# A weight-load counter that starts at three, and one weight split moved ahead of small work, in a two-layer encoder trunk

## The chip, the core and the metric

The kernel runs on one core of a Trainium2 chip. The core has TensorE (PE; its weight loads are shown as PEld), VectorE (DVE), ScalarE (ACT), GpSimd (POOL) and SyncE (SP, here only an issuer of DMAs). Each engine takes its instructions in the order in which the program was written for it. The metric is the time of one execution on the device in microseconds. A change of the time is told apart from none, for this kernel, only if it is above about 0.3%.

## What is computed

The input is x of 256 positions by 2048 features, in float32. Two layers are applied, each an attention with a residual and then a squared-ReLU MLP with a residual; between them one shared key/value projection is made for the second layer.

```
u = rms_norm(h, a_norm_g);  proj = u @ a_w_in            # q, k, v and 16 forget gates
q, k = rms_norm per head;   logf = log_sigmoid(fz + b_f) # layer a: 16 heads of 128
s = q k^T * scale + c[t] - c[s]   (c = cumsum logf, causal);  o = softmax(s) v
h = h + o @ a_w_out;  h = h + relu(rms_norm(h) @ w1)^2 @ w2       # 2048 -> 8192 -> 2048
k_sh, v_sh = rms_norm(h) @ kv_w                                    # shared by layer b
q = rms_norm(rms_norm(h) @ b_w_q);  s = q k_sh^T * scale + rel_bias (own chunk + 8 before)
h = h + softmax(s) v_sh @ b_w_out;  h = h + relu(rms_norm(h) @ w1')^2 @ w2'
```

About 0.5 GB of float32 weights are read once, and every weight has to be multiplied at float32 accuracy.

## The kernel before, in words

**Stages.** The program is one straight stream. In the profiled execution the q/k/v projection of layer a with its attention lies at about 0 to 290 us, the projection after the attention (`w_oa`) up to about 380, the MLP of layer a and the query projection of layer b up to about 1045, the shared key/value projection with the attention of layer b and its output projection up to about 1405, and the MLP of layer b to the end.

**Units and splits.** Weights are worked through in units of 128x1024 float32 elements. A unit is split by ACT into a rounded part `hi` (L339) and by DVE into the rest `lo` (L340); PE then makes three passes with it, `hi` by the high part of the activations (L608), `hi` by their low part (L610) and `lo` by the high part (L612), four matmuls of 512 columns in each pass. `hi` and `lo` have three buffers each. So the split of a unit can start only when PE has done with the unit three before it: `hi` is free after the L610 pass and `lo` after the L612 pass.

**Pairs and forms.** Two panels of 512 output columns make a pair. Part of the products of a pair is saved by a seven-product scheme for 2x2 blocks: instead of eight block products there are seven, on sums of the weight blocks. These sums are called forms (names "11", "T3", "T2", "T1", "21", "T4", "22" of L157). Some sums are made by DVE (L990, L992), others by a DMA from POOL's queue that adds a second weight block into the tile where the first lies (L1005, L1007). In layer a the q/k/v projection after the first few panels goes in four pairs of the kind "three": their forms are 1536 columns wide, that is three couples of 256-row blocks. Such a form is worked in two items, first its 1024 columns (6 matmuls) and at once after that the other 512 (3 matmuls, tiles `half`); only the first is a full unit with buffers of `hi` and `lo`. Between the forms stand narrow units, of 12 matmuls each.

**Order of the work.** `plan_heads` and `plan_mlp` write down a list of items (pair, kind, number): kind 0 or 1 is a narrow unit of one of the two panels, kind 2 the first part of a form, kind 3 the second. `run` (L1025) goes through that list. At each narrow unit `fetch` calls `top_up` (L356), which splits ahead until three full units are split and not yet given to PE, and loads ahead until three raw units (four within the MLPs) wait in SBUF. Then come the unit's 12 matmuls, and after them `run_fill` (L1061) takes the next entry of a queue of small work, as often as the table `HM` says for that item. The small work is softmax, head norms, transposes through DRAM (`carry`: rows to DRAM from SP at L466, columns back at L472), the second layer's sums and so on. At a form of a "three" pair nothing is split ahead first: the form's own unit is popped, and one unit more is split only after the form's second part (`top_up(AHEAD - 1)`). All of this gives the order in which the instructions stand on PE, DVE, ACT and SP, and that order is kept.

**Where a loaded unit lies.** `load` (L300) issues the DMA of the next narrow unit on SP (L310). It counts its calls in `extra[1]`. Within the MLPs (`extra[0]` is true) each load whose count is divisible by five does not go into one of the four buffers `raw` but into one of the two buffers of the tag `z`, as `zraw`. The same two buffers take in turn the transposed tiles `z` of the hidden panels and of h; these leave by 16 small DMAs from SP and POOL (`hop`, L482) or through DRAM (L466, L472).

```
extra[1] += 1
raw = qkv.tile([P, UN], F32, name="zraw", tag="z", bufs=2) if extra[0] and extra[1] % 5 == 0 else wraw.tile([P, UN], F32, name="raw")
```

## Time and profile before

| | |
|---|---|
| median of 3 runs | 2062.64 us (2061.12 to 2068.23) |
| the profiled execution, its own time | 2057.46 us |
| its span from first to last instruction | 2055.7 us |
| PE busy | 2044.0 us, 99% of the span, 9048 matmuls |
| DVE busy | 1786.3 us, 87% |
| ACT busy | 1410.1 us, 69% |
| DMA | 560.92 MB, mean 273 GB/s |
| granted TensorE clock | 1.00 |

The profiled execution is shorter than the median by 5.2 us. A busy share is an average over the whole span. A row of the profile names the line of the kernel, the engine, the operation and "output<-input" tiles; brackets and arrows give the idle time of that engine before it and what ended that idle time. Matmuls are pipelined: one of 512 columns is shown as about 390 ns long, but in an undisturbed stream four follow each other in some 0.91 us. So a wait of PE that is short against the modelled length of a matmul can be hidden in its row.

### The profile page before, as it was taken

What the parts mean: (1) busy time and instruction counts of PE and PEld (TensorE: products, weight loads), DVE (VectorE), ACT (ScalarE), POOL (GpSimd) and SP (SyncE); (2) the same over time, 40 slices, a digit from 0 to 9 for tenths busy, and PEclk for the clock granted to TensorE, in tenths of its full rate; (3) what the DMA queues carried; (4) which work ended last, traced back from release to release, by engine and by line L of the source; (5) the groups of instructions that cost most, each with busy time, mean ns of one, the idle gap of its engine ahead of it and who ended that gap; (6) DMA issues with size and microseconds to landing.
All of it is one profiled execution on the core that took longest, in us unless ns stands there. A gap on an engine that the chain in (4) does not pass through costs nothing.

```text
span 2055.7 us, 27156 instructions
## 1 busy us (share of the span) xinstructions
PE 2044.0 (99%) x9048; PEld 1684.3 (82%) x9048; DVE 1786.3 (87%) x2099; ACT 1410.1 (69%) x1826; POOL 252.4 (12%) x359
## 2 busy tenths in 40 slices
PE   9999999999999999999999999999999999999999
PEld 8887878877888888888788888888788888888887
DVE  7888888898898899898888787888988988988996
ACT  7776666677677676667678666667766676776764
POOL 1222110011111102101012111100111111111020
PEclk9999999999999999999999999999999999999999
DMA  8899997998888898898889988878988888888985
GB/s 322 275 282 290 298 294 238 307 271 263 292 260 285 259 296 275 243 293 260 267 246 296 282 256 280 259 253 286 294 290 266 266 265 293 261 286 255 301 259 149
DMA packets 177901, 560.92 MB, mean 273 GB/s; under 512 B 40912, under 2 KB 69472, under 8 KB 155232
## 3 DMA queue, kind: packets, MB, share of 16 engines
q1 hardware_dynamic: 155552, 466.04, 63.7%
q0 software_dynamic: 21920, 92.84, 23.0%
q8 instruction: 71, 1.16, 0.2%
q14 instruction: 70, 0.57, 0.1%
q10 hardware_dynamic: 288, 0.30, 0.0%
HBM read 519.22 MB, written 27.29 MB: 266 GB/s over the span
## 4 chain that ended last, share of the span: by engine, by line
PE 89%; DMA 4%; issue 3%; DVE 2%; ACT 1%; SPq 0%; POOL 0%; DVEq 0%; ACTq 0%; POOLq 0%
PE acc L612 21%; PE acc L608 21%; PE acc L610 21%; PE s L612 8%; PE s L608 8%; PE s L610 8%; DVE lo L340 1%; DMA turn<-z 1%; PE po L745 1%; PE po L776 1%; ACT hi L339 1%; DMA wT<-in_w1fa 1%; DMA w<-in_w1fb 0%; DMA z<-turn 0%; DMA raw<-in_w1sb 0%
## 5 line engine op out<-in xcount | busy, mean ns | idle before, releaser
L339 ACT ACTIVATE hi<-raw 128x1024 fp32r<-128x1024 f32 (+1 forms) x401 | 421.5, 1054 | 197.3 <-PE acc L610 128.9
L340 DVE TENSOR_TENSOR lo<-raw,hi 128x1024 fp32r<-128x1024 f32 (+1 forms) x401 | 485.2, 1213 | 70.5 <-ACT hi L339 65.0
L608 PE MATMUL acc<-hi,act 128*128 128x512 f32 x1750 | 490.6, 393 | 2.7 <-ACT hi L339 2.6
L612 PE MATMUL acc<-lo,act 128*128 128x512 f32 x1750 | 484.8, 390 | 1.1 <-DVE lo L340 0.8
L610 PE MATMUL acc<-hi,act 128*128 128x512 f32 x1750 | 484.2, 389 | 0.0
L612 PEld LDWEIGHTS acc<-lo,act 128*128 128x128 f32 x1750 | 327.8, 188 | 72.4 <-DVE lo L340 4.5
L608 PEld LDWEIGHTS acc<-hi,act 128*128 128x128 f32 x1750 | 326.5, 188 | 71.7 <-ACT hi L339 4.8
L610 PEld LDWEIGHTS acc<-hi,act 128*128 128x128 f32 x1750 | 328.4, 188 | 69.2 <-DVE act L399 0.5
L339 ACT ACTIVATE hi<-w 128x1024 fp32r<-128x1024 f32 x254 | 266.9, 1058 | 124.6 <-PE acc L610 83.8
L340 DVE TENSOR_TENSOR lo<-wT,hi 128x1024 fp32r<-128x1024 f32 x220 | 267.1, 1221 | 63.7 <-ACT hi L339 59.8
L340 DVE TENSOR_TENSOR lo<-w,hi 128x1024 fp32r<-128x1024 f32 x254 | 305.6, 1219 | 17.4 <-ACT hi L339 15.7
L339 ACT ACTIVATE hi<-wT 128x1024 fp32r<-128x1024 f32 x220 | 232.2, 1060 | 102.5 <-PE acc L610 44.2
L608 PE MATMUL s<-hi,act 128*128 128x512 f32 x522 | 144.7, 392 | 0.5 <-ACT hi L339 0.5
L612 PE MATMUL s<-lo,act 128*128 128x512 f32 x522 | 143.3, 389 | 0.1
L610 PE MATMUL s<-hi,act 128*128 128x512 f32 x522 | 142.7, 388 | 0.0
L482 POOL DMA_DIRECT2D q<-z x192 | 95.7, 513 | 254.1 <-DVE z L456 212.5
L612 PEld LDWEIGHTS s<-lo,act 128*128 128x128 f32 x522 | 97.3, 188 | 21.8 <-DVE lo L340 2.0
L608 PEld LDWEIGHTS s<-hi,act 128*128 128x128 f32 x522 | 97.5, 188 | 21.3 <-ACT hi L339 1.4
L610 PEld LDWEIGHTS s<-hi,act 128*128 128x128 f32 x522 | 97.8, 188 | 20.4
L608 PE MATMUL s<-hi,S 128*128 128x512 f32 x288 | 89.1, 390 | 0.0
L612 PE MATMUL s<-lo,S 128*128 128x512 f32 x288 | 88.7, 389 | 0.0
L610 PE MATMUL s<-hi,S 128*128 128x512 f32 x288 | 88.7, 389 | 0.0
(246 smaller groups left out, 2375.6 us busy)
## 6 DMA issues: line engine op xcount, KB each, us to landing
w<-in_w2fa SPq DMA_DIRECT2D x32, 1024.0 KB, 6.3
w<-in_w2fb SPq DMA_DIRECT2D x32, 1024.0 KB, 6.4
w<-in_w1fa SPq DMA_DIRECT2D x27, 1024.0 KB, 7.9
w<-in_w1fb SPq DMA_DIRECT2D x27, 1024.0 KB, 7.3
raw<-in_w2sb SPq DMA_DIRECT2D x52, 512.0 KB, 7.4
raw<-in_w2sa SPq DMA_DIRECT2D x51, 512.0 KB, 7.6
raw<-in_w_kv SPq DMA_DIRECT2D x48, 512.0 KB, 5.4
raw<-in_w1sa SPq DMA_DIRECT2D x45, 512.0 KB, 6.1
```

What stands on the lines that cost most here:

```text
L339: S.activation(hi[:, c], raw[:, c], AF.Copy)
L340: V.tensor_tensor(lo[:, c], raw[:, c], hi[:, c].bitcast(F32), op=ALU.subtract)
L482: (G if i % 2 else SY).dma_start(dst[32 * j : 32 * j + 32, i * n : (i + 1) * n], z[32 * i : 32 * i + 32, j * n : (j + 1) * n])
L608: TE.matmul(ps[:, cols], xh, cut(hi, j), start=first, stop=False, **kw)
L610: TE.matmul(ps[:, cols], xl, cut(hi, j), start=False, stop=False, **kw)
L612: TE.matmul(ps[:, cols], xh, cut(lo, j), start=False, stop=last, **kw)
L745: TE.matmul(s[:, P : 3 * P], q[:, a, P:T], k[:, a], start=True, stop=True)
L776: TE.matmul(po[:, :T], v[:, 0, a * P : (a + 1) * P], pT[:, :2], start=True, stop=False)
```

## The change

The count of loads starts at three in place of zero. And in `run`, after the matmuls of a narrow unit and before its small work, `top_up()` is called if the next item of the list is the first part of a form of a "three" pair.

```
-    extra = [False, 0]
+    extra = [False, 3]
...
                 if p.fast and (q, u) == (0, p.own) and not early_v:
                     join_v(p)
+                then = plan[i + 1] if i + 1 < len(plan) else (p, 0, 0)
+                if then[1] == 2 and then[0].order == "three":
+                    top_up()
                 for _ in range(1 if masks is None else masks[i]):
                     run_fill()
```

PE's order is the same in both kernels. On the other engines these three places show what moves.

ACT at the end of the last "three" pair (about 263 to 276 us of the profiled execution), before: `hi<-R` is the split of form "11" of the output projection's first pair, `sq` and `qn` are the norm of the last keys, `S<-sum` and `q<-z` other small work.

```order
L339 ACTIVATE hi<-raw 128x1024
L780 ACTIVATE act<-po 128x256
L418 ACTIVATE S<-sum 128x512 x2
L711 ACTIVATE q<-z,gqk 128x1024
L676 ACTIVATE sq<-acc 128x512 x2
L339 ACTIVATE hi<-R 128x1024
L690 ACTIVATE qn<-acc,ss 128x128 x4
L339 ACTIVATE hi<-raw 128x1024
```

The same place in the changed kernel:

```order
L339 ACTIVATE hi<-raw 128x1024
L339 ACTIVATE hi<-R 128x1024
L780 ACTIVATE act<-po 128x256
L418 ACTIVATE S<-sum 128x512 x2
L711 ACTIVATE q<-z,gqk 128x1024
L676 ACTIVATE sq<-acc 128x512 x2
L690 ACTIVATE qn<-acc,ss 128x128 x4
L339 ACTIVATE hi<-raw 128x1024
```

The split `hi<-R` went ahead of six pieces of small work; the split `hi<-raw` behind the keys' norm stayed behind it.

DVE at the first head's softmax (about 94 to 102 us), before: L759 to L456 end that head's softmax and transpose it, L753 begins the next head's.

```order
L340 TENSOR_TENSOR lo<-raw,hi 128x1024
L759 RECIPROCAL row<-row 128x2
L761 TENSOR_SCALAR pbuf<-pbuf,row 128x128
L761 TENSOR_SCALAR pbuf<-pbuf,row 128x256
L456 STREAM_TRANSPOSE pbuf<-pbuf 128x3x4x32
```

The same place in the changed kernel:

```order
L340 TENSOR_TENSOR lo<-raw,hi 128x1024
L340 TENSOR_TENSOR lo<-wT_852,hi 128x1024
L759 RECIPROCAL row<-row 128x2
L761 TENSOR_SCALAR pbuf<-pbuf,row 128x128
L761 TENSOR_SCALAR pbuf<-pbuf,row 128x256
L456 STREAM_TRANSPOSE pbuf<-pbuf 128x3x4x32
```

The row `lo<-wT`, which stood behind the next head's L753 rows before, now stands ahead of the end of this head's softmax.

SP near the start of layer a's MLP (about 365 to 395 us), before: `raw` and `zraw` are loads of narrow units, `q<-turn` and `turn<-z` a transpose through DRAM, `w` tiles take blocks for forms.

```order
L310 DMA raw<-in_w1a 128x1024 x2
L310 DMA zraw<-in_w1a 128x1024
L472 DMA q<-turn 32x4x256 x4
L310 DMA raw<-in_w1a 128x1024 x2
L949 DMA w_3610<-in_w1fa 128x2048
L310 DMA raw<-in_w1a 128x1024 x2
L466 DMA turn<-z 128x1024
L946 DMA w_3688<-in_w1fa 128x1024
L310 DMA zraw<-in_w1a 128x1024
```

The same place in the changed kernel:

```order
L310 DMA raw<-in_w1a 128x1024 x3
L472 DMA q<-turn 32x4x256 x4
L310 DMA raw<-in_w1a 128x1024
L310 DMA zraw<-in_w1a 128x1024
L949 DMA w_3610<-in_w1fa 128x2048
L310 DMA raw<-in_w1a 128x1024 x2
L466 DMA turn<-z 128x1024
L946 DMA w_3688<-in_w1fa 128x1024
L310 DMA raw<-in_w1a 128x1024
```

The loads themselves and their order are the same; which of them goes into a `z` buffer has moved. Counted from the first such load of an MLP, the sequence in layer a was two `raw`, one `zraw`, then four and one; it is now four and one from the start, which is the sequence that layer b's MLP had before. Layer b's MLP now has one `raw`, one `zraw`, then four and one, which neither MLP had.

## The prediction, as put on record

> **What bounds the kernel now.** I read the page first, then busy time by stage, then PE's waits stage by stage.

> ```profile
> span 2055.7 us, 27156 instructions
> PE 2044.0 (99%) x9048; PEld 1684.3 (82%) x9048; DVE 1786.3 (87%) x2099; ACT 1410.1 (69%) x1826; POOL 252.4 (12%) x359
> PEclk9999999999999999999999999999999999999999
> ```

> PE works in 99% of the span at the full granted clock, and the change takes no matmul away. So a gain can come only from PE's waits, 2055.7 - 2044.0 = 11.7 us in all. By stage (heads of layer a, its output projection, its MLP, heads of layer b, its MLP), the first figure after the length is PE's busy time:

> ```profile
> 89.00:287.00 198.00, 195.78 (x876) 159.81 (x876) 168.85 (x276) 136.34 (x246) 36.63 (x37) 1.00 0.90 276
> 287.00:380.00 93.00, 92.64 (x415) 76.52 (x415) 78.20 (x112) 60.19 (x94) 1.75 (x2) 1.00 0.83 265
> 380.00:1045.00 665.00, 662.06 (x2905) 543.65 (x2904) 596.19 (x598) 459.96 (x502) 77.05 (x129) 1.00 0.88 274
> 1045.00:1405.00 360.00, 359.94 (x1621) 298.97 (x1620) 298.39 (x440) 248.21 (x411) 45.00 (x43) 1.00 0.86 267
> 1405.00:2056.00 651.00, 646.12 (x2849) 532.90 (x2847) 574.79 (x570) 440.26 (x466) 75.41 (x127) 1.00 0.86 269
> ```

> The moved split acts in the first row, with 198.00 - 195.78 = 2.2 us of idle PE, and a little beyond; the counter acts in the third and fifth, with 2.9 and 4.9 us. What PE waited for, from 89 to 380 us (five rows), in layer a's MLP (two) and in layer b's (one):

> ```profile
> PE po L744 <- DMA R<-turn: 1.2, 1, 1.2
> PE s L608 <- ACT hi L339: 0.5, 1, 0.5
> PE po L776 <- DMA pbuf<-turn: 0.3, 1, 0.3
> PE po L744 <- PE acc L612: 0.2, 1, 0.2
> PE acc L608 <- ACT act L780: 0.2, 1, 0.2
> ...
> PE acc L608 <- ACT hi L339: 2.1, 3, 0.9
> PE acc L612 <- DVE lo L340: 0.6, 1, 0.6
> ...
> PE acc L612 <- DVE lo L340: 0.2, 1, 0.2
> ```

> 2.4, 2.7 and 0.2 us: the rest of layer b's 4.9 us is, for the most part, no wait for another engine but the end of the program. All that the change can touch is thus 5.3 us, under the 0.3% (6.2 us) that a measurement of this kernel can tell from no change.

> **Part one, the split moved ahead of small work.** Of the 2.4 us only one row, 0.5 us, is a wait for a split. The others wait for transposes through DRAM or for the evacuation of an attention matmul. This is the place, on ACT and then on PE:

> ```profile
> 263.25 1.04 ACT L339 ACTIVATE hi<-raw 128x1024 fp32r<-128x1024 f32 x1
> 267.45 0.38 ACT L780 ACTIVATE act<-po 128x256 fp32r<-128x256 f32 x1 [3.16 <-PE po L777]
> 270.48 1.06 ACT L676 ACTIVATE sq<-acc 128x512 f32<-128x512 f32 x2
> 271.43 1.06 ACT L339 ACTIVATE hi<-R 128x1024 fp32r<-128x1024 f32 x1
> 273.19 1.14 ACT L690 ACTIVATE qn<-acc,ss 128x128 f32<-128x128 f32 x4 [0.71 <-POOL ss L684]
> 274.21 1.07 ACT L339 ACTIVATE hi<-raw 128x1024 fp32r<-128x1024 f32 x1
> ...
> 275.33 1.20 PE L608 MATMUL s<-hi,act 128*128 128x512 f32 x4 [0.52 <-ACT hi L339]
> ```

> Before 267.45 ACT stands idle for 3.16 us, and the moved `hi<-R` of 1.06 us goes into that hole. At first sight this mends the wait at 275.33. But that wait is for the next split, `hi<-raw` of 274.21, and in the new order this one still stands behind the four `qn`, which wait for POOL until 273.19. Their chain starts with `sq` at 270.48, which the move does not bring forward. `hi<-R` comes 5 us earlier; what is late next is the same `hi<-raw`, at the same time. So I take nothing for it. If `hi<-raw` did come earlier the gain would be the 0.5 us of the row, and with the 0.2 us of L744 behind it, which hangs on the same keys, 0.7.

> The cost: the small work now stands behind one split at each of the places, seven forms in each of four pairs. A split takes 1.06 us of ACT and about 1.2 of DVE. It could also hold up its engine until PE releases its buffers, but in this stage splits seldom wait for PE, unlike in the MLP (first two rows: 89 to 287 us; last two: 380 to 1045):

> ```profile
> ACT hi L339 <- PE acc L610: 4.7, 7, 1.1
> ACT hi L339 <- PE s L610: 2.7, 2, 1.6
> ...
> ACT hi L339 <- PE acc L610: 112.4, 147, 1.7
> ACT hi L339 <- PE s L610: 46.8, 72, 1.2
> ```

> 7.4 us in nine waits, against 159.2. ACT and DVE run behind PE here, so that a split moved forward mostly finds its buffers free and costs its own length: the small work is later by about 1.2 us and has caught up after the form, where that split is missing. Who waits for it? At the first head, DVE's transpose ends the softmax, SP sends the rows out, then the columns back, and PE needs them:

> ```profile
> 96.50 0.58 DVE L456 STREAM_TRANSPOSE pbuf<-pbuf 128x384 f32<-128x384 f32 x1
> 97.11 0.33 SPq L466 DMA_DIRECT2D turn<-pbuf  x1
> L472 SPq DMA_DIRECT2D pbuf<-turn x4: 326/430/432, 99.0 to 100.3; - x4
> DMA to landing us min/median/max: 1.7/1.9/5.7
> 107.23 0.59 PE L776 MATMUL po<-pbuf,R 128*128 128x256 f32 x2
> ```

> The last of the four was issued at 100.3, and with the slowest landing of 5.7 the tile is there at 106.0, 1.2 us before PE's 107.23. The `lo` now ahead of the softmax's end costs DVE 1.2: just covered. At the late ones (`R<-turn` 1.2 us, `pbuf<-turn` 0.3) the delay would show at once if DVE or ACT set the time of the rows, up to one unit of PE each. Three passes of about 0.91 us make 2.7 for that unit. Value taken: 0, with the bounds -0.7 and +2.7 (one such place late by a whole unit).

> **Part two, the count from three.** It adds no instruction. It changes which loads wait for a `z` buffer on SP and which for `raw`, and by that when each 512 KB transfer is issued. Loads themselves have room:

> ```profile
> DMA to landing us min/median/max: 3.7/7.0/14.3
> ...
> DMA to landing us min/median/max: 3.6/7.8/13.8
> ```

> These are the `zraw` loads of layers a and b, and no PE wait above names a load. What does make PE wait is a form built by POOL's adding DMA, which shares the DMA engines with the loads:

> ```profile
> 913.86 0.85 POOL L1005 DMA_DIRECT2D wT<-in_w1fa  x1 [18.93 <-DVE Sh L421]
> 925.66 2.01 ACT L339 ACTIVATE hi<-wT 128x1024 fp32r<-128x1024 f32 x2 [4.35 <-DMA wT<-in_w1fa]
> 1009.71 2.01 ACT L339 ACTIVATE hi<-wT 128x1024 fp32r<-128x1024 f32 x2 [3.11 <-DMA wT<-in_w2fa]
> 433.46 1.06 ACT L339 ACTIVATE hi<-wT 128x1024 fp32r<-128x1024 f32 x1 [2.66 <-DMA wT<-in_w1fa]
> ```

> Issued at 913.86 and used at 925.66: 11.8 us. Such a landing hangs on what else is in the queues, so the position of `zraw` can decide it. Here the trace holds a comparison. Layer a gets the sequence that layer b has now, and layer b, with nearly the same work, has PE waits of 0.2 us. If the sequence is all that matters, layer a loses 2.7 - 0.2 = 2.5 us of waits; if the place matters (layer a's MLP runs into a query projection, layer b's does not), nothing. Halfway: -1.2. Layer b gets a sequence not seen: between the 0.2 and the 2.7 seen, if sequence matters, a mean of +1.25, or 0 if not; halfway +0.6. The bounds are -2.5 and 0 for layer a, -0.2 and +2.5 for layer b.

> **Sum.** Against the profiled execution's 2057.46 (span 2055.7 and 1.8 around it): 0 - 1.2 + 0.6 = -0.6, that is 2056.8. The median of the runs stands 5.2 us above the profiled execution; 2062.64 - 0.6 = 2062.0. Bounds: -0.7 - 2.5 - 0.2 = -3.4, and 2.7 + 0 + 2.5 = +5.2.

> **Rivals.**

> *The moved split blocks the small work (slower).* It decides if the split waits, at the head of ACT's and DVE's order, for PE to end the unit just given, rather than finding its buffers free. Then each small step behind it is late by 2.7 us and not 1.2. The price at four tight places: the first head 2.7 - 1.2 = 1.5; the two DMA rows above and the keys of L744, already late, 2.7 each: 9.6, so 2057.46 + 9.6 = 2067.1, or 2072.2 on the median's scale. Against it stand the nine waits above. It decides once the first head's rows go out later than 97.11 + 1.2 = 98.3. [...] Chance 0.08.

> *All touched waits vanish (faster).* 2057.46 - 5.3 = 2052.2, or 2057.3 on the median's scale: still 0.26%, inside 0.3%. It takes a part of the 5.2 us between profile and median as well, if these are late landings of the same kind. Chance 0.06.

> *The change does nothing.* The split stands earlier in the text but starts when it did, and the landings do not care for the sequence: 2062.6. For it speaks the `hi<-raw` at 274.21. Chance 0.20.

> *The sequence is bad in both MLPs.* Layer a keeps its 2.7, layer b gets 2.7: +2.5, 2065.1. Chance 0.12. Against it stands layer b's present 0.2.

> **How the numbers follow.** The forecast, a shift within the bounds that cannot be told from none, has 0.54. It, the last rival (0.12) and "nothing" (0.20) lie within 0.3% of 2062.64 (2056.5 to 2068.8): 0.86. Faster 0.06, slower 0.08. The range: 2062.0 with the bounds -3.4 and +5.2 around 2062.64 is 2059.2 to 2067.8; runs of one kernel lie from 2061.12 to 2068.23 and the profiled one at 2057.46, so I take 2056.5 to 2068.

> **What would show it.** Right: ACT's `hi<-R` starts near 266 instead of 271.43, yet PE still waits for `hi<-raw` near 275; the first head's rows leave by 98.3; PE's waits in layer a's MLP fall below 2.7 us, and in layer b's they stay under that. Wrong: a PE wait on L776 or L744 above 2 us in layer a's heads (the blocking), or many new waits for `wT` tiles in an MLP. The forecast falls if PE's busy time stays at 2044 and the idle time changes by more than 6 us.

## The result

The changed kernel is slower. Its median is 2071.14 us (2067.0 to 2072.14, seven runs) against 2061.63 us of the kernel before (2059.51 to 2068.23, seven runs, the three of the first table among them): 9.5 us by the medians, and a ratio of 1.0039 with a 95% interval of 1.0029 to 1.0049. The profiled execution took 2067.0 us, against 2057.46. In both cases the profiled execution is a short one, by 4 to 5 us, so the two profiles may be compared with each other. From the page of the changed kernel, first the span, then TensorE's busy time, then its busy tenths in 40 slices of 51.6 us:

```profile
span 2065.2 us, 27159 instructions
...
PE 2045.1 (99%) x9048; PEld 1686.3 (82%) x9048; DVE 1785.9 (86%) x2099; ACT 1411.1 (68%) x1826; POOL 250.8 (12%) x359
...
PE   9999989999999999999999999999999999999999
```

PE's idle time went from 11.7 to 2065.2 - 2045.1 = 20.1 us, and the one slice below 9 is the sixth, 258 to 310 us: the end of layer a's heads. The same five stages as in the prediction, with the borders moved by PE's lag (to within four matmuls):

```profile
90.00:298.20 208.20, 197.89 (x877) 161.05 (x876) 170.40 (x280) 137.69 (x246) 33.88 (x37) 0.99 0.87 265
298.20:392.00 93.80, 92.60 (x416) 76.52 (x415) 78.19 (x112) 60.06 (x94) 1.74 (x2) 1.00 0.83 267
392.00:1056.40 664.40, 662.11 (x2909) 544.77 (x2908) 596.94 (x599) 461.23 (x503) 77.06 (x129) 1.00 0.89 274
1056.40:1415.50 359.10, 359.10 (x1617) 298.25 (x1616) 297.61 (x439) 247.41 (x410) 45.06 (x43) 1.00 0.88 271
1415.50:2065.20 649.70, 645.43 (x2849) 533.33 (x2847) 574.34 (x570) 439.61 (x466) 75.39 (x127) 1.00 0.86 267
```

The heads took 208.2 us instead of 198.0, with 10.3 us of idle PE instead of 2.2 and a mean granted clock of 0.99 instead of 1.00. The other stages kept their length within 1.3 us. PE's waits for others in the heads (the four longest of six rows), in the output projection (two) and in layer a's MLP (three):

```profile
PE po L776 <- DMA pbuf<-turn: 5.1, 2, 2.7
PE acc L608 <- ACT sq L676: 1.7, 1, 1.7
PE po L744 <- DMA R<-turn: 1.4, 1, 1.4
PE acc L608 <- ACT pbuf L757: 1.4, 1, 1.4
...
PE po L744 <- DMA R<-turn: 1.0, 1, 1.0
PE acc L608 <- ACT act L780: 0.2, 1, 0.2
...
PE acc L608 <- ACT hi L339: 0.8, 1, 0.8
PE acc L608 <- DVE acc L1047: 0.7, 1, 0.7
PE acc L612 <- DVE lo L340: 0.6, 1, 0.6
```

PE's order is the same in both kernels, so each matmul of the one can be set beside the same matmul of the other. The lag below is the start of a matmul in the changed kernel less its start in the kernel before; a step in it is where time was lost. What comes before 89 us and in the MLPs differs from execution to execution: the lag at 89 us is 1.1 us here and lies between -0.2 and 1.9 in the profiles of the next section, also where nothing was moved up to there; the MLPs follow below.

| matmul, start in the kernel before | lag behind it | step |
|---|---|---|
| start of the stage, 89 us | 1.1 us | |
| `acc<-hi,S`, 104.94 | 2.35 | +1.26 |
| `hi`, `lo` and `half` at 114 to 137 | 4.0 | +1.7 in small steps |
| L776 at 142.47, L744 at 156.78 | 3.75 | -0.58, +0.21 |
| `s<-lo` 190.63, `acc<-hi,S` 197.02 | 6.2 | +0.52, +1.82 |
| L776 at 266.61 and at 272.17 | 11.55 | +2.52, +2.75 |
| L744 at 290.81 | 12.1 | +0.84 |
| end of layer a's MLP, 1045 | 10.6 | -1.6 |
| end of the program | 9.55 | -1.0 |

So 11.0 us were lost between 89 and 291 us, where the moved split acts, most of it at two kinds of places.

**Sums that PE waits for.** At 104.94 and 197.02 PE goes on into an accumulator that DVE still has to add up (L1047). Of DVE before, of DVE after, and of PE before and after:

```profile
104.10 0.69 DVE L1047 SCALAR_TENSOR_TENSOR acc<-acc,p 128x512 f32<-128x512 f32 x1
```

```profile
103.50 1.22 DVE L340 TENSOR_TENSOR lo<-R,hi 128x1024 fp32r<-128x1024 f32 x1
...
105.42 0.58 DVE L456 STREAM_TRANSPOSE pbuf<-pbuf 128x384 f32<-128x384 f32 x1
...
106.45 0.69 DVE L1047 SCALAR_TENSOR_TENSOR acc<-acc,p 128x512 f32<-128x512 f32 x1
```

```profile
104.94 0.70 PE L608 MATMUL acc<-hi,S 128*128 128x512 f32 x2
...
107.29 0.70 PE L608 MATMUL acc<-hi,S 128*128 128x512 f32 x2 [1.37 <-ACT pbuf L757]
```

The sum starts 2.35 us later, 1.09 of which PE was late itself, so 1.26 late against PE. It stands behind the softmax's end, and the moved `lo<-R` now stands ahead of both. The profile names ACT's L757 as releaser, but what ended last is the sum: 106.45 + 0.69 = 107.14, and PE goes on 0.15 us later. In the kernel before, too, PE went on 0.15 us after the end of the sum, 104.10 + 0.69 = 104.79: the sum had no slack, although the profile names no wait there. At 197.02 the same sum stands behind the same kind of rows; PE goes on 0.14 us after its end in the changed kernel and 0.15 us in the kernel before.

**The transposes of the last pair.** DVE's transpose of the probabilities and of the keys, and SP's rows out, before and after:

```profile
250.66 0.58 DVE L456 STREAM_TRANSPOSE pbuf<-pbuf 128x384 f32<-128x384 f32 x1
...
251.69 0.70 DVE L456 STREAM_TRANSPOSE z<-qn 128x512 f32<-128x512 f32 x1
```

```profile
252.42 0.33 SPq L466 DMA_DIRECT2D turn<-z  x1
252.80 0.42 SPq L466 DMA_DIRECT2D turn<-pbuf  x1
```

```profile
258.85 0.58 DVE L456 STREAM_TRANSPOSE pbuf<-pbuf 128x384 f32<-128x384 f32 x1
...
259.88 0.71 DVE L456 STREAM_TRANSPOSE z<-qn 128x512 f32<-128x512 f32 x1
```

```profile
256.63 7.15 SPq L310 DMA_DIRECT2D raw<-in_w_ins  x2
263.83 0.77 SPq L466 DMA_DIRECT2D turn<-z  x1
264.65 0.47 SPq L466 DMA_DIRECT2D turn<-pbuf  x1
```

PE's own lag there is 6.2 us. Against PE, DVE's transpose is late by 258.85 - 250.66 - 6.2 = 2.0 us, but SP's rows by 264.65 - 252.80 - 6.2 = 5.65. The rest arises on SP: the moved split also brought the next loads forward, and the second of the two loads in the 7.15-us row was issued only at 263.46 in the trace; the rows behind it waited, although `z` was ready at 259.88 + 0.71 = 260.6. In the kernel before the rows of `z` left within 0.1 us of their transpose and those of `pbuf` right behind. The way through DRAM was longer, too: the rows of `pbuf` took 6.4 us to land, for 3.8 before. So the last columns of this head landed at 275.18; before they had landed at 262.10, 4.5 us ahead of PE's 266.61. The next head had no such room. Its last columns landed at 272.08 before, 0.1 us ahead of PE:

```profile
272.17 0.67 PE L776 MATMUL po<-pbuf,R 128*128 128x256 f32 x2
```

In the changed kernel SP sent this head's rows only at 275.74, behind the columns of the head ahead (sent at 271.12, for 256.64 before), and their columns landed at 283.63, 0.1 us before PE went on at 283.72.

**A split that is not ready.** Of the small steps the last ones, 0.6 us at `half` (136.4 to 136.9), come from a third kind of place. From 130.6 us in the trace ACT stood 3.26 us at the moved `hi<-R`, until the load of that block had landed; the keys' `sq` and `qn` and that `half` stood behind it. In the kernel before `sq` came first, and `hi<-R` found its block there. What made the other small steps is not shown.

**The granted clock.** After the second of the two long stops the clock fell to half. Three windows of the changed kernel (their length, PE's busy time, and after the five engines the granted clock), then PE's rows:

```profile
281.00:282.00 1.00, 0.00 (x1) 0.00 (x0) 0.16 (x1) 1.00 (x3) 0.00 (x0) 1.00 0.28 66
284.90:288.30 3.40, 3.40 (x10) 2.61 (x9) 2.95 (x4) 3.40 (x9) 1.39 (x3) 0.51 0.81 294
288.40:291.40 3.00, 3.00 (x15) 2.46 (x14) 2.97 (x3) 0.82 (x1) 0.00 (x0) 1.00 0.79 200
```

```profile
283.72 0.67 PE L776 MATMUL po<-pbuf,R 128*128 128x256 f32 x2 [2.71 <-DMA pbuf<-turn]
...
286.55 1.91 PE L608 MATMUL s<-hi,act 128*128 128x512 f32 x4
```

For 3.4 us four matmuls take 1.91 us where they take 1.07 to 1.20 elsewhere. At half the clock 3.4 us hold 1.7 us less work; that is an upper bound on the loss. Over this stretch the lag grew by only 0.3 us, since the kernel before lost time at these matmuls, too (its wait at 275.33 among others); over most of the stretches in the profiles of the next section it grew by 1.2 to 1.8 us. Averaged over the runs, the granted clock of the changed kernel was 0.9977 and that of the kernel before 0.9991 (27 runs of the next section), which is 4.7 against 1.8 us per run. By this estimate at most about 3 of the 9.5 us are lost clock, and the rest is waits. In the two profiles compared here most of the lag is waits.

### The profile page after: what moved, and what is told of

Same layout as the page of the kernel before. It is cut to its first block, busy times and chain, and to the rows that moved or that the text cites. A ratio compares the mean times of both kernels' runs of the same rounds, so it can differ in the third digit from the quotient of the medians.

```text
span 2065.2 us, 27159 instructions
## 1 busy us (share of the span) xinstructions
PE 2045.1 (99%) x9048; PEld 1686.3 (82%) x9048; DVE 1785.9 (86%) x2099; ACT 1411.1 (68%) x1826; POOL 250.8 (12%) x359
## 4 chain that ended last, share of the span: by engine, by line
PE 85%; DMA 2%; DVE 1%; ACT 1%; issue 1%; SPq 0%; POOL 0%; DVEq 0%; ACTq 0%; POOLq 0%
PE acc L608 20%; PE acc L612 20%; PE acc L610 20%; PE s L612 8%; PE s L608 8%; PE s L610 8%; DVE lo L340 1%; DMA q<-z 1%; DMA w<-in_w2fa 1%; PE po L745 1%; PE po L776 1%; DMA zraw<-in_w2sa 0%; DMA R<-turn 0%; DMA turn<-z 0%; ACT hi L339 0%
## 5 line engine op out<-in xcount | busy, mean ns | idle before, releaser
L339 ACT ACTIVATE hi<-raw 128x1024 fp32r<-128x1024 f32 (+1 forms) x401 | 421.0, 1054 | 193.4 <-PE acc L610 126.5
L340 DVE TENSOR_TENSOR lo<-raw,hi 128x1024 fp32r<-128x1024 f32 (+1 forms) x401 | 485.6, 1216 | 77.3 <-ACT hi L339 72.6
L608 PE MATMUL acc<-hi,act 128*128 128x512 f32 x1750 | 490.6, 393 | 1.5 <-ACT hi L339 1.2
L612 PE MATMUL acc<-lo,act 128*128 128x512 f32 x1750 | 485.0, 390 | 0.8 <-DVE lo L340 0.6
L610 PE MATMUL acc<-hi,act 128*128 128x512 f32 x1750 | 484.7, 390 | 0.0
L612 PEld LDWEIGHTS acc<-lo,act 128*128 128x128 f32 x1750 | 328.2, 188 | 71.9 <-DVE lo L340 3.5
L610 PEld LDWEIGHTS acc<-hi,act 128*128 128x128 f32 x1750 | 328.5, 188 | 69.3 <-DVE act L399 0.5
L608 PEld LDWEIGHTS acc<-hi,act 128*128 128x128 f32 x1750 | 326.6, 188 | 70.2 <-ACT hi L339 3.3
L339 ACT ACTIVATE hi<-w 128x1024 fp32r<-128x1024 f32 x254 | 266.8, 1058 | 126.0 <-PE acc L610 83.2
L340 DVE TENSOR_TENSOR lo<-wT,hi 128x1024 fp32r<-128x1024 f32 x220 | 267.1, 1222 | 66.0 <-ACT hi L339 62.9
L340 DVE TENSOR_TENSOR lo<-w,hi 128x1024 fp32r<-128x1024 f32 x254 | 305.7, 1220 | 17.1 <-ACT hi L339 15.4
L339 ACT ACTIVATE hi<-wT 128x1024 fp32r<-128x1024 f32 x220 | 231.7, 1060 | 106.5 <-PE acc L610 45.9
L608 PE MATMUL s<-hi,act 128*128 128x512 f32 x522 | 145.2, 393 | 0.0
L612 PE MATMUL s<-lo,act 128*128 128x512 f32 x522 | 143.0, 389 | 0.4 <-DVE lo L340 0.4
L610 PE MATMUL s<-hi,act 128*128 128x512 f32 x522 | 142.7, 388 | 0.0
L612 PEld LDWEIGHTS s<-lo,act 128*128 128x128 f32 x522 | 97.6, 188 | 21.4 <-DVE lo L340 1.3
L608 PEld LDWEIGHTS s<-hi,act 128*128 128x128 f32 x522 | 98.2, 189 | 20.2
L610 PEld LDWEIGHTS s<-hi,act 128*128 128x128 f32 x522 | 98.0, 188 | 20.4
L608 PE MATMUL s<-hi,S 128*128 128x512 f32 x288 | 89.0, 390 | 0.0
L612 PE MATMUL s<-lo,S 128*128 128x512 f32 x288 | 88.8, 389 | 0.0
L610 PE MATMUL s<-hi,S 128*128 128x512 f32 x288 | 88.7, 389 | 0.0
```

Of the source, the lines that this page charges most:

```text
L339: S.activation(hi[:, c], raw[:, c], AF.Copy)
L340: V.tensor_tensor(lo[:, c], raw[:, c], hi[:, c].bitcast(F32), op=ALU.subtract)
L608: TE.matmul(ps[:, cols], xh, cut(hi, j), start=first, stop=False, **kw)
L610: TE.matmul(ps[:, cols], xl, cut(hi, j), start=False, stop=False, **kw)
L612: TE.matmul(ps[:, cols], xh, cut(lo, j), start=False, stop=last, **kw)
```

## The experiments

Each kernel below was timed in five rounds beside the kernel before. All ratios are to that kernel; one thousandth is 2.06 us.

| kernel | median, us | ratio, 95% interval |
|---|---|---|
| count from three alone | 2060.48 | 1.0001 [0.9986, 1.0016] |
| moved split alone | 2069.26 | 1.0036 [1.0024, 1.0049] |
| moved split, loads stay | 2070.96 | 1.0040 [1.0023, 1.0057] |
| moved split, not ahead of form number 2 | 2068.91 | 1.0037 [1.0024, 1.0051] |
| split behind the small work | 2063.64 | 1.0005 [0.9994, 1.0016] |
| moved split, all pairs but the last | 2065.16 | 1.0019 [1.0007, 1.0031] |
| moved split, last pair alone | 2066.54 | 1.0016 [1.0003, 1.0029] |
| mirror image, all forms | 2067.94 | 1.0026 [1.0015, 1.0038] |
| mirror image, last pair | 2065.29 | 1.0018 [1.0006, 1.0031] |
| mirror image, last pair, all units | 2069.49 | 1.0036 [1.0023, 1.0049] |
| mirror image, `half` early, all forms | 2065.92 | 1.0021 [1.0011, 1.0032] |
| mirror image, `half` early, last pair | 2060.87 | 0.9988 [0.9979, 0.9997] |

**Which of the two parts.** First the count alone, then the split alone with the count from zero.

```
-    extra = [False, 0]
+    extra = [False, 3]
```

> Only the count of loads starts at three; no split is moved. Theory: the whole loss of the changed kernel (9.5 us between the two profiled executions) lies in the heads of layer a and comes from the moved split, while the count gains about 2.6 us in the two MLPs (PE's lead over the kernel before falls from 12.1 us at 303 us to 9.5 us at the end). Then this kernel takes about 2059 us beside 2061.6 of the kernel before, and its heads of layer a are as before. Rival: those 2.6 us are chance landings; then it takes 2061.6, within 1 us of the kernel before, with PE waits of some 2.9 us in the two MLPs.

```
+                then = plan[i + 1] if i + 1 < len(plan) else (p, 0, 0)
+                if then[1] == 2 and then[0].order == "three":
+                    top_up()
                 for _ in range(1 if masks is None else masks[i]):
                     run_fill()
```

> Only the split is moved ahead of the small work; the count starts at zero. Theory: plus 11 to 12 us, 2073 us, with PE waits for transposes (L776, L744) and before the form T1 in layer a's heads, as in the changed kernel, and the MLPs as in the kernel before. Rival, that count and split act only together: about 2066 us or less.

The moved split alone makes the loss, 7.4 us by the ratio where 11 to 12 were expected; the count alone makes no difference that can be measured. In the profile the lag of the count's kernel fell by 3.0 us within layer a's MLP, and that of the changed kernel by 1.6. But it fell there by 3.8, 0.5 and 0.9 us too in the moved-split kernels of this section whose count starts at zero: the profiled execution of the kernel before happened to lose more in that MLP than others do.

**The loads that move with the split.** Here `top_up` splits at the new place but loads nothing, so that ACT's and DVE's orders are those of the moved split and SP's is that of the kernel before.

```
-    def top_up(ahead=AHEAD, early=EARLY):
+    def top_up(ahead=AHEAD, early=EARLY, loads=True):
...
-        while units and sum(1 for r in raws if r[1]) < early + extra[0]:
+        while loads and units and sum(1 for r in raws if r[1]) < early + extra[0]:
...
+                    top_up(loads=False)
```

> As split_only, but the call that splits ahead of the small work issues no loads: ACT's and DVE's orders are those of split_only to the last row, SP's order is that of the kernel before. Loads theory: in the changed kernel SP stands at a load that waits for a raw buffer while the rows of a transpose behind it are ready, and in the last three-couple pair that alone makes 6.1 us (2.5 and 2.8 at L776, 0.8 at L744). Then this kernel is 5 to 6 us faster than split_only, about 2067, and the waits on L776 near 270 and 280 us fall under 0.5. Splits theory (rival): the transposes are late because ACT and DVE reach them late, whatever SP does; then it takes the same 2073 as split_only.

The loads are not the cause: 1.0040 without them, 1.0036 with them. SP's rows for the head at 266.61, and then two of PE's waits in the stage:

```profile
261.57 0.33 SPq L466 DMA_DIRECT2D turn<-z  x1
261.95 0.42 SPq L466 DMA_DIRECT2D turn<-pbuf  x1
```

```profile
PE po L776 <- DMA pbuf<-turn: 3.0, 2, 2.6
PE acc L608 <- ACT sq L676: 1.7, 1, 1.7
```

The rows do leave 2.7 us earlier than in the changed kernel (261.95 against 264.65). Against PE, whose lag is 7.2 us there, they are late by the 2.0 us of DVE's transpose and no more, and that head's wait is gone. But the next head waits 2.6 us: its rows left 1.0 us late against PE and took 7.6 us to land, for 5.6 in the kernel before, where the columns had landed 0.1 us ahead of PE. The sums wait as in the changed kernel, and so the time does not change. The 3.7 us that SP added above are real, but they were not what the total hung on. Why that transfer took 2.0 us longer is not shown.

**One of the sites taken out.** The sum at 104.94 is made behind the form with number 2 of its pair. Here the moved split is left out ahead of the forms with that number alone.

```
-                if then[1] == 2 and then[0].order == "three":
+                if then[1] == 2 and then[0].order == "three" and then[2] != 2:
```

> As split_only, but nothing is split ahead before form T1 (number 2), so that DVE's sum of the accumulator (L1047), which PE needs for the next form, no longer stands behind a split of that form. Theory: the waits of 1.3 us at 107 and 1.8 us at 203 of the changed kernel are this; both go, and the kernel takes about 2070, 3 us less than split_only, while the waits at L776 and L744 stay. Rival: those waits come from the other moved splits; then the time is that of split_only, 2073.

The step at 104.94 went and the one at 197.02 fell from 1.82 to 0.70, yet the time stayed at 1.0037: the 3 us that were expected of it did not come. Two of PE's waits in the stage:

```profile
PE po L776 <- DMA pbuf<-turn: 4.2, 2, 2.3
PE s L608 <- ACT half L339: 2.9, 1, 2.9
```

The second one is new. It lies at 136.43 in the time of the kernel before. ACT's `half` stands there behind the keys' `sq` and `qn`, and these behind the moved `hi<-R`, which stood 4.73 us until its load had landed (3.26 in the changed kernel). Behind this wait PE ran at half the clock for 3.4 us. So what was saved at one form was lost at another in this execution.

**Position or amount.** The same call, behind the small work instead of ahead of it:

```
                 for _ in range(1 if masks is None else masks[i]):
                     run_fill()
+                then = plan[i + 1] if i + 1 < len(plan) else (p, 0, 0)
+                if then[1] == 2 and then[0].order == "three":
+                    top_up()
```

> Edit: the same call of top_up, under the same condition, stands behind the loop that runs the small work instead of ahead of it; the count starts at 0. So as many units are split early, only behind the form's small work and ahead of its evacuation and of what is prepared next. Theory A (order: the loss comes from small work that stands behind a split of 1.05 us on ScalarE or 1.22 us on VectorE): the softmax, the transposes and the norms keep their places, the waits for pbuf<-turn near 275 and 283 us go away, and the time is that of the kernel before, within 3 us (2059 to 2065). The sums of L1047 still stand behind one more split where they are made in the evacuation, so up to 2 us of the loss may stay. Theory B (amount: it is the one unit more that is split early, wherever it stands, which holds buffers and brings the reads of the next rows forward): the loss stays at 7 to 11 us (2068 to 2072).

1.0005: as fast as the kernel before, within an interval of -1.2 to +3.3 us. As many units are split ahead of the forms; only the small work keeps its place. PE's four longest waits in the stage:

```profile
PE po L744 <- DMA R<-turn: 2.5, 2, 1.4
PE s L608 <- ACT hi L339: 1.5, 1, 1.5
PE acc L608 <- DVE acc L1047: 1.0, 1, 1.0
PE po L776 <- DMA pbuf<-turn: 1.0, 1, 1.0
```

The two transposes of the last pair wait 1.0 us instead of 5.1. PE still waits 1.0 and 0.9 us for the two sums L1047, as expected: they are made in the evacuation, which the split now precedes. In the profiled execution, which is the median one here, PE lost 5.0 us up to 303 us against the profile of the kernel before (a short execution); the count alone lost 2.0 there, the moved split alone 13.0. So some loss may be left, at most 3.3 us by the interval, and its interval and that of the moved split (1.0024 to 1.0049) do not meet. This is the run that decides for order against amount.

**Where in the stage.** The moved split in all pairs but the last, and in the last alone:

```
-                if then[1] == 2 and then[0].order == "three":
+                if then[1] == 2 and then[0].order == "three" and then[0].at != 10:
```

> Edit: the moved split everywhere but in the last of layer a's pairs (at == 10); the count starts at 0. From the two profiles aligned matmul by matmul, the last pair holds waits of 2.5 and 2.75 us on pbuf<-turn (L776), 0.8 us on R<-turn (L744) and one stretch of 3.4 us at half the granted clock (1.7 us), 7.8 us together; the pairs before it hold 1.26 + 0.75 + 1.82 + 0.52 us less 0.4, some 4 us. Theory A (each site costs by itself): slower than before by 3 to 5 us (2064.5 to 2066.5). Theory C (the last pair's transposes alone: what is late earlier is caught up): as before, within 1.5 us. Theory D (PE's lateness earlier only shifts the same loss to the end): as the moved split everywhere, slower by 7 us or more.

> Edit: the moved split in the last of layer a's pairs only (at == 10); the count starts at 0. Theory A (each site costs by itself): slower than before by 4 to 7 us (2065 to 2068), with PE's waits for pbuf<-turn of some 2.5 us near 275 and 283 us in the trace, and a stretch at half the clock behind one of them. Theory C (last pair alone): 7 to 9 us. Theory D (the delay gathers over the pairs, and without the earlier ones the last pair is on time): within 1.5 us of before.

3.9 and 3.3 us by the ratios, 7.2 together, against 7.4 for the moved split everywhere: this fits sites that cost by themselves, as theory A said. The intervals are wide, though (1.4 to 6.4 and 0.6 to 6.0 us), so that they do not show the sum, only that neither half is free. The last pair alone waits for no sum, only for transposes, while the kernel without it has both sums (two rows each; it also waits 2.6 us on L744 and 1.4 us on L776 in the pair that it leaves alone):

```profile
PE po L744 <- DMA R<-turn: 4.6, 2, 3.2
PE po L776 <- DMA pbuf<-turn: 3.1, 2, 2.1
```

```profile
PE acc L608 <- ACT pbuf L757: 1.9, 1, 1.9
PE acc L608 <- ACT sq L676: 1.7, 1, 1.7
```

One step I had counted for the last pair can't be. L744 at 290.81 also lost 2.4 us in the kernel that leaves the last pair as it was, and 1.2 in that with the count alone. How late `R<-turn` lands there differs between executions whatever the order. L776 at 272.17, with its 0.1 us of room, waited 1.4 and 0.9 us in those two kernels, so that part of its 2.75 us is of that kind, too.

**The mirror image.** If small work that is late costs time, small work that is earlier may save some. One unit less is split before the matmuls ahead of a form, and that split comes behind the small work:

```
-            hi, lo = ready.popleft()[:2] if q > 1 and ready and not p.deep else fetch()
+            then = plan[i + 1] if i + 1 < len(plan) else (p, 0, 0)
+            late = q < 2 and then[1] == 2 and then[0].order == "three"
+            hi, lo = ready.popleft()[:2] if q > 1 and ready and not p.deep else fetch(AHEAD - 1) if late else fetch()
...
                     run_fill()
+                if late:
+                    top_up(AHEAD - 1)
```

> Edit, the mirror image of the change: at the item ahead of each form of a "three" pair one unit less is split before the unit's matmuls (fetch(AHEAD - 1)), and the split that is left out comes behind the small work (top_up(AHEAD - 1)); the count starts at 0. The small work ahead of the forms is then earlier by one split than in the kernel before. Theory A (order alone, loss by lateness of small work): the gain can be what PE still waits for there in the kernel before: 1.7 us in its profiled execution (rows L744, L776), some 3 to 4 us in a usual one, which is 4 us longer: 2058 to 2061. Theory E (the place in the kernel before is the balance; a split brought later makes PE wait for hi and lo): new waits of PE for hi L339 and lo L340 of 0.5 to 1 us at several of the 28 places, slower by 3 to 8 us (2065 to 2070).

> Edit: the same mirror image in the last of layer a's pairs only. Theory A: the last pair's L776 and L744 lose their waits, at most 3 us faster (2058.5 to 2062); PE does not wait for pbuf<-turn near 275 us in the trace. Theory E: slower by 1 to 3 us with waits for hi or lo in 235 to 290 us.

> Edit: as the mirror image in the last pair, but at every narrow unit of that pair and not only at those ahead of a form. Theory A: as the one before or up to 1 us better, since more of the small work is earlier (2058 to 2062). Theory E: slower by 1 to 4 us with waits of PE for hi or lo in 235 to 290 us.

All three are slower, by 5.4, 3.7 and 7.4 us by the ratios. The sign is that of theory E, with another tile than it named; the two in the last pair cost more than it said (1 to 3 and 1 to 4 us). In the first:

```profile
PE acc L612 <- DVE half L340: 2.9, 3, 1.5
PE acc L608 <- ACT half L339: 2.5, 2, 1.9
PE s L608 <- ACT half L339: 2.3, 1, 2.3
```

The waits for transposes and sums are gone from the stage, as theory A said, but the remainder of each form (`half`) had come behind the small work too, and PE takes it right after the form's first part. So I split `half` early again and left only the full unit behind it for later, at all forms and then in the last pair alone:

```
+            if late and half_next() and not any(r[2] for r in ready):
+                issue()
             if p.ps is None:
                 open_pair(p)
```

> Edit: the mirror image of the change at every form of the "three" pairs, but the form's 512-column remainder (tiles half) is split ahead of the small work, as in the kernel before; only the full unit behind it comes later. The count starts at 0. In the first mirror image PE waited 7.7 us for half (L339, L340) and no longer for the transposes (L744, L776). Theory A (order; what stands behind what decides): those waits go, the transposes stay early, and the time is that of the kernel before or up to 4 us less: 2057 to 2062, with PE waits under 3 us in 89 to 290 us. Theory E (the order before is the balance): the wait moves on to the late full unit (hi, lo) or to the sums L1047, and the time stays 3 to 7 us above before (2065 to 2069).

> Edit: the same in the last pair only. Theory A: before less 0 to 3 us (2058.5 to 2062); no wait of PE for half near 258 and 272 us, none above 1 us for pbuf<-turn. Theory E: 1 to 4 us above before (2063 to 2066).

At all forms the wait moved on to `hi` (3.1 us at one place) and the kernel is slower. In the last pair alone it is 0.9988 [0.9979, 0.9997]: faster than the kernel before by some 2 us, the only one of these kernels that is. Its largest wait between 230 and 300 us is still one for a split, 2.1 us for `hi`, with a stretch at half the clock behind it.

The interval leaves 1 out, but it is one of twelve kernels, and the gain is well below the 0.3% that a measurement of this kernel is usually taken to tell. The tiles of L776 in the last pair now land 7.0 and 3.4 us before PE needs them, for 4.5 and 0.1 before. But PE itself comes later there: its profiled execution (2059.07 us) is 3.5 us behind that of the kernel before at 303 us. So no profile shows where the gain would come from, and it stays open.

## Why the prediction was wrong

It forecast no change (2062.0 us, 0.86 on "within 0.3%"); the kernel became 0.39% slower. Step by step:

- **What bounds.** PE's idle time as the only place for a gain held. But "all that the change can touch is thus 5.3 us" bounded gains alone: the 8.35 us that are named above at the sums and at the transposes of L776 were no rows of the profile before. The text's last sign came: PE's busy time hardly moved (2045.1 for 2044.0), and its idle time grew by 8.4 us. (2057.46 - 0.6 is 2056.9, not the 2056.8 of the text; nothing hangs on it.)
- **The split in ACT's hole.** `hi<-R` went where I said: 272.14 - 6.2 = 265.9 on the old scale, for "near 266". The wait for `hi<-raw` at 275 did not stay; PE came later than that split, and 0.5 us of the loss was given back there.
- **"The small work is later by about 1.2 us and has caught up after the form."** This is the step that failed. The size was near: 1.26 us at the first sum, 99.06 - 1.09 - 96.50 = 1.5 at the first head's transpose, 2.0 in the last pair, but 5.65 for the rows out behind SP's load. What was wrong is that it costs nothing. PE needed results of the late work before it had caught up: the sums L1047, which the prediction never listed and which had no slack, and the transposes of the last pair, one of which had 0.1 us. With "value taken: 0" and a bound of 2.7 us for one late place, the sum had no room for the eight steps up in the table, 11.0 us net.
- **The first head.** "Just covered" was right, by other numbers: the rows left at 99.66 - 1.09 = 98.6 us, later than the 98.3 of the text, and took 4.9 us to land for 1.9 before; but the slowest columns took 2.7 us for 5.7, and the tile was there at 108.52, 0.9 us before PE's 109.43. The tight rows were the wrong guide, too. At 142.47 (`pbuf<-turn`, 0.3 us of wait before) 0.58 us were gained and at 156.78 (`R<-turn`, 1.2 us) 0.21 lost, while the 5.3 us were lost at two transposes without a row among the waits before.
- **The rival "the moved split blocks the small work",** with chance 0.08, gave 2067.1 us for the profiled execution; it took 2067.0. Both of its signs came: rows of the first head later than 98.3, and waits above 2 us on L776. Part of its mechanism is there. ACT's splits waited for PE 7.4 us in nine waits before; in the changed kernel (90 to 300 us):

```profile
ACT hi L339 <- PE acc L610: 14.8, 15, 2.3
...
ACT hi L339 <- DMA R<-in_w_in: 5.3, 2, 3.3
...
ACT hi L339 <- DVE wT L990: 4.4, 3, 2.3
...
ACT hi L339 <- PE s L612: 1.0, 1, 1.0
```

  15.8 us in 16 waits for PE, and 9.7 us in five for the split's own input, two rows that the kernel before had not. In the longest of these waits, 3.26 us up to 133.82, ACT did nothing else: the keys' `sq` and an `act` of 0.39 us, written behind that split, came only after it, at 134.78 and 135.81. I dismissed the rival by the nine waits of the old order, which say nothing about a split that has been moved to where the unit just given to PE still holds its buffer. But its four places were not those that cost: only L744 at 156.78, with 0.2 us, and at 290.81 are among the steps, and the latter is not the change's. The closeness of the number is chance. How much of the whole loss is the splits' own length and how much their waits was not separated by a run. At the places shown above the moved `lo` on DVE waited 0 us (first sum and first head) and 0.3 us (last pair), so that there its own 1.2 us make most of the delay; at 137 us it is the wait.
- **The count.** The signs (-1.2 in layer a's MLP, +0.6 in layer b's) were neither confirmed nor refuted: 1.0001 with an interval of -2.9 to +3.3 us. The changed kernel's MLP rows (2.1 us of waits in layer a for 2.7; none in layer b) are as the text asked, and the kernels with the old count scatter as widely. "Such a landing hangs on what else is in the queues" holds on average, by less for forms than for loads: in the trace of the kernel before, an adding `wT` transfer issued with at most one other transfer under way took 8.2 us to land (mean of 11) and with two or more 9.5 us (37), a `raw` load with none 3.4 us (8) and with five or more 7.6 us (148).
- **The clock.** The prediction read 1.00 off the page and priced each wait at its own length. In these profiles some stops of about 2 us or more came with 3.4 us at a clock of 0.50, by estimate up to 1.7 us beside the stop.

## What to carry over

A profile shows the waits of the order that it was taken in. To price work that is moved ahead of other work on one engine, list everything that then stands behind it, and for each its next user and the slack in front of that user: the sums and the transpose that were just in time before (no slack, and 0.1 us) have no row among the waits. Ask also whether the moved work is ready at its new place; if it is not, what stands behind it is late, too, as behind the 3.26 us at `hi<-R`. Here small work and splits were both needed soon, and moving the order either way made new waits. Of the moves that split later, only the smallest, a single unit at the forms of one pair, was not slower, and its gain is too small to be sure of.

## What the runs showed of the hardware

Stops of PE shorter than 3.4 us came with a stretch of 3.4 us at half the clock in some places and without one in others. Over the 14 profiles there are 21 single stops of PE between 1.87 and 3.22 us behind the start phase; 13 of them come with a stretch of 3.4 us at a granted clock of 0.50 that begins at most 1.5 us after PE goes on (in two cases it began within the stop, and one of these is two stretches on end), and 8 do not, among them stops of 2.94 and 2.64 us. None of the single stops from 0.8 to 1.8 us is followed by one.

Part of the scatter of the kernel before seems to go with the clock: of its 27 runs beside the first four kernels, the 10 with a mean clock of 1.000 have a median of 2058.9 us and the 7 with 0.998 one of 2064.1.
